# Group states of a Mamba-2 SSD layer: B and the weighted x in a high and a low part, three rounded products in place of plain 32-bit ones, for groups 1 to 7

## The chip, the cores and the metric

The kernel runs on one core of one Trainium2 chip. A core has four compute engines and a queue engine, each of which works off its own list of instructions in the order of that list: PE (TensorE, matrix products into PSUM), DVE (VectorE), ACT (ScalarE), POOL (GpSimd, which here also issues a few DMAs) and SP (which issues the weight loads). Engines wait for each other through semaphores. The metric is the time of one execution in microseconds of the device; 0.2% of this kernel's time, 2 us, is about what a measurement can tell from no change.

## The reference

One layer mixes 256 latent tokens, with 256 context tokens as prefix, by a bidirectional Mamba-2 scan of 8 groups of 4 heads and by a gated MLP. The part at hand is the state of a chunk of 128 tokens, per direction, and the output that is read from it:

```python
acs = jnp.cumsum(a, axis=2)
decay_to_end = jnp.exp(a_tot[:, :, None] - acs)
states = jnp.einsum('bckgn,bckgr,bckgrp->bcgrpn', Bc, decay_to_end, xdt)
...
hT, h_starts = lax.scan(step, h0, (states, a_tot))
...
CB = jnp.einsum('bcqgn,bckgn->bcgqk', Cc, Bc)
y_diag = jnp.einsum('bcgqk,bcgrqk,bckgrp->bcqgrp', CB, Lmat, xdt)
y_off = jnp.einsum('bcqgn,bcgrpn,bcqgr->bcqgrp', Cc, h_starts, jnp.exp(acs))
```

A group's state is a product of B (tokens by 128) with x, each token of x weighted by its decay. B, C and x come from the input projection through a depthwise convolution of width 5 and SiLU.

## The kernel before

The input projection makes 32 channel tiles of 128 channels (for group g: tiles 4g and 4g+1 are x, 4g+2 is B, 4g+3 is C, for which the latent tokens alone are computed). Seven tiles are made in a first stage, the other 25 in the stage with which the change is concerned, from 130 to 432 us: PE adds up 16 steps of k into the PSUM tile `psx`. Each step is three products of numbers in the rounded 32-bit form (`float32r`): a weight w is split into a high part `hi_w` (ACT, a cast) and a low part `lo_w` (DVE, w minus the high part), and high times high, high times low and low times high are summed (`mm3`, lines 139 to 143). The activations stand split in `hhi` and `hlo`. Splits run three half tiles ahead of PE (`split_hi`, `split_lo`, lines 492 to 502).

Between these products the recurrence of the groups runs, by a clock written out by hand: `later(dt, fn)` files a piece of work under a due time, `pump` moves the clock forward by 1.3 for two steps of k (0.65 for a tile of latent tokens) and issues what is due. On PE, DVE, ACT and POOL the instructions stand in the order in which `pump` issues them. Of a tile i (`plan_tile`, line 877) come in turn:

- the convolution (`conv_tile`): ACT starts the sum from `psx` (`tap0`, line 560), DVE adds four taps (line 576), ACT applies SiLU (line 579). The exponential of the decays, `E` (line 743, ACT), needs another table than SiLU, so ACT loads tables in between (ACT_TABLE_LOAD, at lines 579 and 743);
- of an x tile, a transposition on PE (`ptx`, line 695) and a copy to `xk` (`ssd_xc`, line 699, ACT); after the second x tile of a group, `ssd_w` on POOL: four products of `xk` with decays make `xw` (context tokens, line 707), two make `xl` (latent tokens, line 710);
- of a B tile, a transposition (`ptb`, line 718) and a copy to `bk` (line 723, ACT);
- after the C tile, the recurrence of the group: on PE `pcb` (C times B, line 761), `psc` and `psl` (the states, lines 778 and 781, plain 32-bit products, each of which the trace shows as two passes), then `hs` (the states joined: ACT line 788, POOL line 794, DVE line 800), `M` (POOL line 806 and DVE line 814), `E` times M (line 816), `pso` (line 831), `yo` (DVE line 837), the sum of `yo` into `y` (POOL line 845), `psy` (line 857), `yc` (ACT line 864) and `pty` (line 871).

The rows R of decays of the next group are loaded by a DMA that POOL issues (line 677) once `ssd_min` (line 737, DVE) has read those of the group before. `cv1` is a pool with one buffer for each tag, so a tile with the same tag waits until the one before has been read.

Of the kernel before, what the change touches and what calls it, by code (L numbers as in the profile page):

```python
# [44 lines left out]
def tile_hybrid_ssd_mlp(  # L45
# [116 lines left out]
    zt, e = yseg(5)[:, 0:256], yseg(5)[:, 256:512]  # L162
# [9 lines left out]
    def spt(shape, name):  # L172
        return sps.tile(shape, F32, tag="s", name=name)
# [136 lines left out]
    for k in range(KT):  # L310
# [5 lines left out]
        g = k % 4  # L316
        nc.tensor.matmul(pss[32 * g : 32 * g + 32, :], lhsT=ones[:, 0:32], rhs=sq, start=k < 4, stop=k >= KT - 4)
        if g == 3:
            warm(512)
            if k < 12:  # L320
# [7 lines left out]
                     start=True, stop=True)  # L328
# [141 lines left out]
    cv1 = cvs.enter_context(mkpool(name="cv1", bufs=1))  # L470
# [76 lines left out]
    def conv_tile(i, src, d0, ds):  # L547
        ch = ORDER[i]
        lat = ch >= 24
        n = 256 if lat else 512  # L550
        cw = pc[:, C_CW + 5 * i : C_CW + 5 * i + 5]
        l0 = 0 if lat else 256
        T = {}

        def tap0():
            if ch < 16:
                o = cv3.tile([P, n], F32, tag="xs", name=f"xbc{i}")
            else:
                o = cv2.tile([P, n], F32, tag="cs" if lat else "bs", name=f"xbc{i}")
            nc.scalar.activation(o, src, AF.Identity, bias=pc[:, C_CB + i : C_CB + i + 1], scale=cw[:, 2:3])  # L560
            T["o"] = o

        def taps():
            o = T["o"]
            o4 = o[:, l0 : l0 + 256].rearrange("p (r t) -> p r t", r=4)
            src4 = src[:, l0 : l0 + 256].rearrange("p (r t) -> p r t", r=4)
            for k in (0, 1, 3, 4):
                s = k - 2
                parts = [(o4, src4, 64)]
                if not lat:  # L570
                    parts.append((o[:, 0:256], src[:, 0:256], 256))
                for (a, z, w) in parts:
# [3 lines left out]
                    nc.vector.scalar_tensor_tensor(ao, zi, cw[:, k : k + 1], ao, op0=ALU.mult, op1=ALU.add)  # L576

        def silu():
            nc.scalar.activation(T["o"], T["o"], AF.Silu)
# [102 lines left out]
    gs_ = {}  # L682

    def hp(ap):
        return ap.rearrange("p (h q) -> p h q", h=4)

    def ssd_x(g, xi):
        S = gs_.setdefault(g, {})
        if xi == 0:
            S["xk"] = cv2.tile([P, 4, 256], F32, tag="xk", name=f"xk{g}")  # L690
        xk = S["xk"]
        xt = done.pop(4 * g + xi)
        p = spt([P, 4, P], f"ptx{g}{xi}")
        for t in range(4):
            nc.tensor.transpose(p[:, t, :], xt[:, t * P : (t + 1) * P], ident)
        S["ptx", xi] = p

    def ssd_xc(g, xi):
        nc.scalar.copy(gs_[g]["xk"][:, :, xi * P : (xi + 1) * P], gs_[g]["ptx", xi])

    def ssd_w(g):
        S = gs_[g]
        xk, h4 = S["xk"], slice(4 * g, 4 * g + 4)
        xw = cv1.tile([P, 2, 2, 256], F32, tag="xw", name=f"xw{g}")
        for t in range(2):
            for d in range(2):
                nc.gpsimd.tensor_tensor(hp(xw[:, t, d, :]), hp(xk[:, t, :]), bc(wctx(t, d)[:, h4], 2, 64), op=ALU.mult)
        xl = cv1.tile([P, 2, 256], F32, tag="xl", name=f"xl{g}")
        for d in range(2):
            nc.gpsimd.tensor_tensor(hp(xl[:, d, :]), hp(xk[:, 2 + d, :]), bc(wlt(d)[:, h4], 2, 64), op=ALU.mult)  # L710
        S["xw"], S["xl"] = xw, xl

    def ssd_b(g):
        bt = done[4 * g + 2]
        bk = cv1.tile([P, 4, P], F32, tag="bk", name=f"bk{g}")
        p = spt([P, 4, P], f"ptb{g}")
        for t in range(4):
            nc.tensor.transpose(p[:, t, :], bt[:, t * P : (t + 1) * P], ident)
# [54 lines left out]
    def ssd_states(g):  # L773
        S = gs_[g]
        bk, xw, xl = S["bk"], S["xw"], S["xl"]
        psc = spt([P, 2, 256], f"psc{g}")
        for t in range(2):
            nc.tensor.matmul(psc, lhsT=bk[:, t, :], rhs=xw[:, t], start=t == 0, stop=t == 1)  # L778
        psl = spt([P, 2, 256], f"psl{g}")
        for d in range(2):  # L780
            nc.tensor.matmul(psl[:, d, :], lhsT=bk[:, 2 + d, :], rhs=xl[:, d, :], start=True, stop=True)
# [307 lines left out]
    for blk in range(16):  # L1089
# [83 lines left out]
    for i in range(8):  # L1173
        tk, b = divmod(i, 4)
# [5 lines left out]
    xf = [load_raw(xtok[tk], f"xf{tk}") for tk in range(2)]  # L1180
# [148 lines left out]
```

## Time and profile before

| | |
|---|---|
| median of 3 runs | 990.47 us (990.31 to 990.49) |
| the profiled execution's own time | 989.67 us |
| its span, first to last instruction | 987.9 us |
| busy: PE, DVE, ACT, POOL | 978.8, 621.4, 495.4, 112.5 us |
| granted clock of PE, mean | 0.999 |

The profile is of one execution. Its page gives each engine's busy time, the chain of work that ended last, and groups of instructions by line; the trace behind it can be asked for a stretch of time, for one line, or for the waits. In a timeline a row has the start in us, the time taken, engine, line, operation, tile written and tiles read; in brackets stands how long the engine had been idle and which work ended that. A matrix product's end is modelled, so the time from its start to the start of the next one is what it costs PE. Rows of equal instructions that follow each other are put together (x4).

### The profile page before, as it was taken

To read this page: it belongs to the slowest core of one execution; us is meant where nothing else is said; L and a number is where in the kernel's file an instruction comes from. 1 tells how busy PE (TensorE), PEld (TensorE's weight loads), DVE (VectorE), ACT (ScalarE), POOL (GpSimd) and SP (SyncE) were. 2 spreads that over 40 slices of the span, in tenths; PEclk is the share of its full clock that TensorE was granted. 3 is DMA by queue.
4 is the path that set the end of the run, shared out by engine and by line. 5 is a ranking of instruction groups with operands and counts; after the bars stand their busy time and mean duration, and the time that the engine had idled before them with its cause. 6 is when DMAs were issued, how large, how long until landed. Compare 5 with 4: busy or idle time off the path is not lost.

```text
span 987.9 us, 13929 instructions
## 1 busy us (share of the span) xinstructions
PE 978.8 (99%) x5502; PEld 792.6 (80%) x5502; DVE 621.4 (63%) x949; ACT 495.4 (50%) x762; POOL 112.5 (11%) x162
## 2 busy tenths in 40 slices
PE   9999999999999999999999999999999999999997
PEld 4688888778887878787888888887888888888885
DVE  4444488868886566756767766767555564445636
ACT  4233358566665554545445343454565563346522
POOL 0000002432453222224000000000000000000000
PEclk9999999999999999999999999999999999999999
DMA  9999844233323424145877768774455446556722
GB/s 372 421 418 418 352 149 166 86 129 128 128 75 139 142 98 145 43 169 206 297 302 284 275 257 296 280 274 170 170 180 203 171 170 213 178 206 228 282 86 85
DMA packets 31985, 207.26 MB, mean 210 GB/s; under 512 B 4128, under 2 KB 4384, under 8 KB 8496
## 3 DMA queue, kind: packets, MB, share of 16 engines
q1 hardware_dynamic: 29232, 192.79, 52.0%
q0 software_dynamic: 2112, 12.65, 3.7%
q8 instruction: 43, 0.70, 0.3%
q10 hardware_dynamic: 576, 0.94, 0.3%
q14 instruction: 22, 0.18, 0.1%
HBM read 204.20 MB, written 2.16 MB: 209 GB/s over the span
## 4 chain that ended last, share of the span: by engine, by line
PE 92%; DMA 4%; ACT 2%; DVE 1%; SPq 0%; issue 0%; ACTq 0%
PE pa L1108 12%; PE pa L1110 12%; PE pa L1109 12%; PE psx L141 9%; PE psx L143 9%; PE psx L142 9%; PE pm L1157 3%; PE pm L1155 3%; PE pm L1156 3%; DMA wst<-in_wst_dram 3%; PE pq L1157 2%; PE pq L1156 2%; PE pq L1155 2%; PE psada L249 2%; PE psc L778 1%; PE pso L831 1%
## 5 line engine op out<-in xcount | busy, mean ns | idle before, releaser
L85 DVE TENSOR_TENSOR lo_w<-w,hi_w 128x1024 fp32r<-128x1024 f32 x173 | 210.7, 1224 | 146.0 <-ACT hi_w L84 145.9
L84 ACT CAST hi_w<-w 128x1024 fp32r<-128x1024 f32 x173 | 182.1, 1053 | 204.5 <-PE pa L1110 129.4
L1108 PE MATMUL pa<-hi_w,hhi 128*128 128x512 f32 x512 | 202.3, 395 | 0.0
L1110 PE MATMUL pa<-hi_w,hlo 128*128 128x512 f32 x512 | 199.5, 390 | 0.0
L1109 PE MATMUL pa<-lo_w,hhi 128*128 128x512 f32 x512 | 199.3, 389 | 0.0
L141 PE MATMUL psx<-hhi,hi_w 128*128 128x512 f32 (+1 forms) x400 | 153.4, 383 | 0.0
L143 PE MATMUL psx<-hhi,lo_w 128*128 128x512 f32 (+1 forms) x400 | 145.9, 365 | 0.0
L142 PE MATMUL psx<-hlo,hi_w 128*128 128x512 f32 (+1 forms) x400 | 145.7, 364 | 0.0
L1108 PEld LDWEIGHTS pa<-hi_w,hhi 128*128 128x128 f32 x512 | 96.2, 188 | 20.5 <-issue 1.6
L1110 PEld LDWEIGHTS pa<-hi_w,hlo 128*128 128x128 f32 x512 | 96.1, 188 | 20.3
L1109 PEld LDWEIGHTS pa<-lo_w,hhi 128*128 128x128 f32 x512 | 96.2, 188 | 19.5 <-issue 0.2
L576 DVE SCALAR_TENSOR_TENSOR xbc<-psx,pc,xbc 128x248 f32<-128x248 f32 (+1 forms) x204 | 83.6, 473 | 34.8 <-ACT xbc L560 33.9
L501 DVE TENSOR_TENSOR lo_w<-w,hi_w 128x1024 fp32r<-128x1024 f32 x61 | 77.1, 1271 | 23.7 <-ACT hi_w L495 23.6
L141 PEld LDWEIGHTS psx<-hhi,hi_w 128*128 128x128 f32 x400 | 75.5, 189 | 13.4 <-issue 2.9
L143 PEld LDWEIGHTS psx<-hhi,lo_w 128*128 128x128 f32 x400 | 75.4, 188 | 12.5
L142 PEld LDWEIGHTS psx<-hlo,hi_w 128*128 128x128 f32 x400 | 75.6, 189 | 12.2 <-issue 1.7
L495 ACT CAST hi_w<-w 128x1024 fp32r<-128x1024 f32 x61 | 63.5, 1044 | 26.0 <-PE psx L142 12.9
L966 DVE SCALAR_TENSOR_TENSOR junk<-gate,cb 128x2048 bf16<-128x2048 f32 x16 | 36.7, 2291 | 24.1 <-DMA gate<-in_wada_dram 24.1
L1155 PE MATMUL pm<-hi_w,hhi 128*128 128x512 f32 x128 | 50.0, 390 | 0.0
L1156 PE MATMUL pm<-lo_w,hhi 128*128 128x512 f32 x128 | 49.9, 390 | 0.0
L1157 PE MATMUL pm<-hi_w,hlo 128*128 128x512 f32 x128 | 49.7, 389 | 0.0
L730 ACT ACTIVATE R<-R,y 128x128 f32<-128x128 f32 x128 | 38.8, 391 | 0.0
(248 smaller groups left out, 1333.6 us busy)
## 6 DMA issues: line engine op xcount, KB each, us to landing
w<-in_wlat_dram SPq DMA_DIRECT2D x64, 1024.0 KB, 4.8
w<-in_wout_dram SPq DMA_DIRECT2D x32, 1024.0 KB, 4.8
ada<-in_wada_dram SPq DMA_DIRECT2D x30, 1024.0 KB, 13.4
w<-in_wxbc_dram SPq DMA_DIRECT2D x25, 1024.0 KB, 4.8
gate<-in_wada_dram SPq DMA_DIRECT2D x16, 1024.0 KB, 5.5
R<-acs POOLq DMA_DIRECT2D x8, 1024.0 KB, 5.2
wst<-in_wst_dram SPq DMA_DIRECT2D x15, 480.0 KB, 14.0
xT<-in_xch_dram SPq DMA_DIRECT2D x4, 1024.0 KB, 8.0
```

Of the source, the lines that this page charges most:

```text
L84: nc.scalar.copy(hi, raw)
L85: nc.vector.tensor_tensor(lo, raw, hi.bitcast(F32), op=ALU.subtract)
L141: nc.tensor.matmul(ps, lhsT=whi, rhs=hhi[k][:, s], start=start, stop=False)
L142: nc.tensor.matmul(ps, lhsT=whi, rhs=hlo[k][:, s], start=False, stop=False)
L143: nc.tensor.matmul(ps, lhsT=wlo, rhs=hhi[k][:, s], start=False, stop=stop)
L576: nc.vector.scalar_tensor_tensor(ao, zi, cw[:, k : k + 1], ao, op0=ALU.mult, op1=ALU.add)
L1108: nc.tensor.matmul(pa[tk], lhsT=hhi[k][:, t], rhs=whi[:, w], start=k == 0, stop=False)
L1109: nc.tensor.matmul(pa[tk], lhsT=hhi[k][:, t], rhs=wlo[:, w], start=False, stop=False)
L1110: nc.tensor.matmul(pa[tk], lhsT=hlo[k][:, t], rhs=whi[:, w], start=False, stop=k == KT - 1)
L1155: nc.tensor.matmul(p, lhsT=yh[:, t], rhs=whi[:, w], start=j == 0, stop=False)
L1156: nc.tensor.matmul(p, lhsT=yh[:, t], rhs=wlo[:, w], start=False, stop=False)
L1157: nc.tensor.matmul(p, lhsT=yl[:, t], rhs=whi[:, w], start=False, stop=hf == 0 and j == 15)
```

## The change

For groups 1 to 7 B and the weighted x are split as the weights are: ACT casts to a high part, DVE subtracts it to get a low part. Each plain product of `psc` and `psl` becomes three rounded ones (high by high, high by low, low by high). POOL now writes one half at a time of the weighted x into a buffer `xf`, which has one copy: part n=0 and n=1 are the two context chunks, n=2 the latent ones. `ssd_w(g, n)` (POOL) and `ssd_ws(g, n)` (ACT cast, DVE subtraction) alternate, 2.7 units of the clock between parts. So POOL's part n+1 waits until ACT and DVE have read part n, and ACT's cast waits for POOL. The tiles share tags with others: the high and the low part of `xl` take those of `yo`, `hs` that of the low part of `xw`. Group 0 is computed as before. Some due times move: the C tiles with `late` of 10 in the early calls get 12, `tw` (from the transposed x to `ssd_w`) becomes 17 for tile 5 and 6 for tile 17, and the product with the skip weight, `ssd_sk`, comes after the three parts.

```diff
-    def ssd_w(g):
+    def ssd_w(g, n):
         S = gs_[g]
+        if g == 0:
+            if n == 0:
+                S["xw"] = cv1.tile([P, 2, 2, 256], F32, tag="xw0", name="xw")
+                S["xl"] = cv1.tile([P, 2, 256], F32, tag="yo0", name="xl")
+            xf = S["xl"] if n == 2 else S["xw"][:, n]
+        elif n == 0:
+            S["xw"] = [cv1.tile([P, 2, 2, 256], F32R, tag=f"xw{v}", name=f"xw{v}{g}") for v in range(2)]
+        if g and n == 2:
+            S["xl"] = [cv1.tile([P, 2, 256], F32R, tag=f"yo{v}", name=f"xl{v}{g}") for v in range(2)]
         xk, h4 = S["xk"], slice(4 * g, 4 * g + 4)
-        xw = cv1.tile([P, 2, 2, 256], F32, tag="xw", name=f"xw{g}")
-        for t in range(2):
-            for d in range(2):
-                nc.gpsimd.tensor_tensor(hp(xw[:, t, d, :]), hp(xk[:, t, :]), bc(wctx(t, d)[:, h4], 2, 64), op=ALU.mult)
-        xl = cv1.tile([P, 2, 256], F32, tag="xl", name=f"xl{g}")
+        if g:
+            S["xf"] = xf = cv1.tile([P, 2, 256], F32, tag="xf", name=f"xf{g}{n}")
         for d in range(2):
-            nc.gpsimd.tensor_tensor(hp(xl[:, d, :]), hp(xk[:, 2 + d, :]), bc(wlt(d)[:, h4], 2, 64), op=ALU.mult)
-        S["xw"], S["xl"] = xw, xl
+            nc.gpsimd.tensor_tensor(hp(xf[:, d, :]), hp(xk[:, 2 + d if n == 2 else n, :]),
+                                    bc((wlt(d) if n == 2 else wctx(n, d))[:, h4], 2, 64), op=ALU.mult)
+
+    def ssd_ws(g, n):
+        S = gs_[g]
+        if g == 0:
+            return
+        hi, lo = S["xl"] if n == 2 else [v[:, n] for v in S["xw"]]
+        nc.scalar.copy(hi, S["xf"])
+        nc.vector.tensor_tensor(lo, S["xf"], hi.bitcast(F32), op=ALU.subtract)
...
     def ssd_bc(g):
-        nc.scalar.copy(gs_[g]["bk"], gs_[g]["ptb"])
+        hi, lo = (gs_[g]["bk"] + [None])[:2]
+        nc.scalar.copy(hi, gs_[g]["ptb"])
+        if g == 0:
+            return
+        nc.vector.tensor_tensor(lo, gs_[g]["ptb"], hi.bitcast(F32), op=ALU.subtract)
...
+        parts = ((0, 0), (0, 1), (1, 0))
+        if g == 0:
+            parts, xw, xl = ((0, 0),), [xw], [xl]
+        e = len(parts) - 1
         for t in range(2):
-            nc.tensor.matmul(psc, lhsT=bk[:, t, :], rhs=xw[:, t], start=t == 0, stop=t == 1)
+            for n, (a, b) in enumerate(parts):
+                nc.tensor.matmul(psc, lhsT=bk[a][:, t, :], rhs=xw[b][:, t], start=t + n == 0, stop=t == 1 and n == e)
...
         if r == 1:
-            later(d0 + tx + tw, lambda: ssd_w(g))
-            later(d0 + tx + tw + 3, lambda: ssd_sk(g))
+            for n in range(3):
+                later(d0 + tx + tw + 2.7 * n, lambda n=n: ssd_w(g, n))
+                later(d0 + tx + tw + 2.7 * n + 1.3, lambda n=n: ssd_ws(g, n))
+            later(d0 + tx + tw + 7.5, lambda: ssd_sk(g))
...
         if i < 8:
-            plan_tile(i, ps, ds=7, tx=11.5 if i == 4 else 9, tw=12, late=10)
+            plan_tile(i, ps, ds=7, tx=11.5 if i == 4 else 9, tw=17 if i == 5 else 12, late=12)
         else:
-            plan_tile(i, ps, td=1.3 if i < 12 else 0)
+            plan_tile(i, ps, td=1.3 if i < 12 else 0, tw=6 if i == 17 else 1.5)
```

Where the instructions move, three places show. In the rows the first number behind a name is the tile's own (xbc19 is channel tile 19, xf42 is part 2 of group 4, xw04 the high part of group 4, hi_w29 a half tile of weights); what follows the underscore is a buffer, which differs between the two programs. Lines are those of each program's own code: L725 and L726 are the new cast and subtraction, L717 is POOL's weighting, L739 and L742 the split of B.

The first place is ACT before the states of group 1. Before:

```order
L864 COPY yc0_2095<-psy0_2078 128x512
L743 ACT_TABLE_LOAD
L743 ACTIVATE E1_2097<-E1_2097 128x1024
L579 ACT_TABLE_LOAD
L579 ACTIVATE xbc8_2074<-xbc8_2074 128x512
L495 CAST hi_w14_2138<-w7_1890 128x1024
L788 COPY hs1_2169<-psc1_2143 128x2x256
```

And now:

```order
L890 COPY yc0_2092<-psy0_2075 128x512
L725 CAST xw01_2068<-xf10_2070 128x512
L762 ACT_TABLE_LOAD
L762 ACTIVATE E1_2094<-E1_2094 128x1024
L725 CAST xw01_2068<-xf11_2115 128x512
L579 ACT_TABLE_LOAD
L579 ACTIVATE xbc8_2066<-xbc8_2066 128x512
L495 CAST hi_w14_2142<-w7_1890 128x1024
L725 CAST xl01_2144<-xf12_2146 128x512
```

The three casts of group 1 stand among the exponential, the SiLU of tile 8 and the weight cast; in the old order POOL had all of group 1's weighting done earlier, ahead of M01. On PE the places of `pcb1`, `psc1` and `psl1` move from step 10 of tile 9 to step 12, behind `ptx20`; `pso1` from step 2 to step 6 of tile 10.

The second place is the same stretch of group 4, on ACT and on POOL. ACT before:

```order
L864 COPY yc3_2981<-psy3_2966 128x512
L579 ACTIVATE xbc18_2906<-xbc18_2906 128x512
L560 ACTIVATE xbc19_3010<-psx19_2899,pc_87 128x256
L495 CAST hi_w29_3012<-w14_2739 128x1024
L743 ACT_TABLE_LOAD
L743 ACTIVATE E4_2983<-E4_2983 128x1024
L723 COPY bk4_3033<-ptb4_3034 128x512
L579 ACT_TABLE_LOAD
L579 ACTIVATE xbc19_3010<-xbc19_3010 128x256
```

ACT now:

```order
L890 COPY yc3_3039<-psy3_3024 128x512
L725 CAST xw04_3009<-xf40_3011 128x512
L579 ACTIVATE xbc18_2961<-xbc18_2961 128x512
L560 ACTIVATE xbc19_3070<-psx19_2954,pc_87 128x256
L495 CAST hi_w29_3075<-w14_2785 128x1024
L762 ACT_TABLE_LOAD
L762 ACTIVATE E4_3041<-E4_3041 128x1024
L725 CAST xw04_3009<-xf41_3072 128x512
L739 CAST bk04_3098<-ptb4_3100 128x512
L725 CAST xl04_3113<-xf42_3115 128x512
L579 ACT_TABLE_LOAD
L579 ACTIVATE xbc19_3070<-xbc19_3070 128x256
```

The SiLU of tile 19, which `pcb4` reads, now stands behind all three casts. POOL before:

```order
L806 TENSOR_TENSOR M31_2870<-cbb3_2819,dtt_1483 128x512
L707 TENSOR_TENSOR xw4_2872<-xk4_2751,ed_1484 128x256 x4
L710 TENSOR_TENSOR xl4_2877<-xk4_2751,ed_1484 128x256 x2
L823 TENSOR_TENSOR y_68<-xk4_2751,dsk_109 128x256 x2
L845 TENSOR_TENSOR y_68<-y_68,yo30_2916 128x256 x2
L845 TENSOR_TENSOR y_68<-y_68,yo31_2938 128x256 x2
L677 DMA R5_2994<-acs_1485 128x2048
```

POOL now:

```order
L871 TENSOR_TENSOR y_68<-y_68,yo31_2991 128x256 x2
L717 TENSOR_TENSOR xf40_3011<-xk4_2802,ed_1484 128x256 x2
L677 DMA R5_3054<-acs_1485 128x2048
L717 TENSOR_TENSOR xf41_3072<-xk4_2802,ed_1484 128x256 x2
L717 TENSOR_TENSOR xf42_3115<-xk4_2802,ed_1484 128x256 x2
L849 TENSOR_TENSOR y_68<-xk4_2802,dsk_109 128x256 x2
```

The weighting of group 4 has moved behind the sum of `yo31` and around the load of R5. On DVE the six instructions around it read, in order: the weight split lo_w27, the first `ssd_min` of E4, the subtraction for xf40, lo_w28, the second `ssd_min` of E4 (for which R5's load waits), the taps of tile 19; then the sum of `pty3`, the subtraction for xf41, lo_w29, the low part of B, the subtraction for xf42.

The third place is ACT ahead of the B tile of group 5; groups 6 and 7 have the same order. Before:

```order
L699 COPY xk5_3215<-ptx51_3302 128x4x128
L560 ACTIVATE xbc22_3335<-psx22_3244,pc_87 128x512
L495 CAST hi_w35_3337<-w17_3059 128x1024
L495 CAST hi_w36_3377<-w18_3190 128x1024
L579 ACTIVATE xbc22_3335<-xbc22_3335 128x512
```

And now:

```order
L699 COPY xk5_3299<-ptx51_3386 128x4x128
L725 CAST xw05_3398<-xf50_3400 128x512
L560 ACTIVATE xbc22_3418<-psx22_3328,pc_87 128x512
L495 CAST hi_w35_3420<-w17_3135 128x1024
L725 CAST xw05_3398<-xf51_3428 128x512
L495 CAST hi_w36_3463<-w18_3274 128x1024
L725 CAST xl05_3471<-xf52_3473 128x512
L579 ACTIVATE xbc22_3418<-xbc22_3418 128x512
```

The SiLU of tile 22, which `ptb5` reads, stands behind the cast of part 2. Groups 2 and 3 have the pattern too: in group 2 the SiLU of tile 10 (read by `ptb2`) comes behind the cast of xf22, in group 3 the SiLU of tile 16 (read by `ptx40`) behind that of xf31. On DVE the subtraction for xf21 stands behind the taps of tile 10 and lo_w17, the one for xf30 behind the taps of tile 16 and lo_w23, the one for xf51 behind the taps of tile 22 and lo_w35.

More of the change, by code (lines that the diff above doesn't have):

```diff
@@ L699, in ssd_xc @@
         nc.scalar.copy(gs_[g]["xk"][:, :, xi * P : (xi + 1) * P], gs_[g]["ptx", xi])
-    def ssd_w(g):
+    def ssd_w(g, n):
         S = gs_[g]
-        xk, h4 = S["xk"], slice(4 * g, 4 * g + 4)
-        xw = cv1.tile([P, 2, 2, 256], F32, tag="xw", name=f"xw{g}")
-        for t in range(2):
-            for d in range(2):
-                nc.gpsimd.tensor_tensor(hp(xw[:, t, d, :]), hp(xk[:, t, :]), bc(wctx(t, d)[:, h4], 2, 64), op=ALU.mult)
-        xl = cv1.tile([P, 2, 256], F32, tag="xl", name=f"xl{g}")
-        for d in range(2):
-            nc.gpsimd.tensor_tensor(hp(xl[:, d, :]), hp(xk[:, 2 + d, :]), bc(wlt(d)[:, h4], 2, 64), op=ALU.mult)
-        S["xw"], S["xl"] = xw, xl
+        if g == 0:
[7 more added lines that the diff above has]
+            S["xl"] = [cv1.tile([P, 2, 256], F32R, tag=f"yo{v}", name=f"xl{v}{g}") for v in range(2)]
+        xk, h4 = S["xk"], slice(4 * g, 4 * g + 4)
+        if g:
+            S["xf"] = xf = cv1.tile([P, 2, 256], F32, tag="xf", name=f"xf{g}{n}")
+        for d in range(2):
+            nc.gpsimd.tensor_tensor(hp(xf[:, d, :]), hp(xk[:, 2 + d if n == 2 else n, :]),
[7 more added lines that the diff above has]
+        nc.vector.tensor_tensor(lo, S["xf"], hi.bitcast(F32), op=ALU.subtract)
     def ssd_b(g):
         bt = done[4 * g + 2]
-        bk = cv1.tile([P, 4, P], F32, tag="bk", name=f"bk{g}")
+        bk = [cv1.tile([P, 4, P], F32R if g else F32, tag=f"bk{v}", name=f"bk{v}{g}") for v in range(2 if g else 1)]
         p = spt([P, 4, P], f"ptb{g}")
@@ L776, in ssd_states @@
         psc = spt([P, 2, 256], f"psc{g}")
+        parts = ((0, 0), (0, 1), (1, 0))
+        if g == 0:
+            parts, xw, xl = ((0, 0),), [xw], [xl]
+        e = len(parts) - 1
         for t in range(2):
-            nc.tensor.matmul(psc, lhsT=bk[:, t, :], rhs=xw[:, t], start=t == 0, stop=t == 1)
+            for n, (a, b) in enumerate(parts):
+                nc.tensor.matmul(psc, lhsT=bk[a][:, t, :], rhs=xw[b][:, t], start=t + n == 0, stop=t == 1 and n == e)
         psl = spt([P, 2, 256], f"psl{g}")
         for d in range(2):
-            nc.tensor.matmul(psl[:, d, :], lhsT=bk[:, 2 + d, :], rhs=xl[:, d, :], start=True, stop=True)
+            for n, (a, b) in enumerate(parts):
+                nc.tensor.matmul(psl[:, d, :], lhsT=bk[a][:, 2 + d, :], rhs=xl[b][:, d, :], start=n == 0, stop=n == e)
         S["psc"], S["psl"] = psc, psl
@@ L786, in ssd_hc @@
         S = gs_[g]
-        S["hs"] = cv1.tile([P, 2, 2, 256], F32, tag="hs", name=f"hs{g}")
+        S["hs"] = cv1.tile([P, 2, 2, 256], F32, tag="xw1", name=f"hs{g}")
         nc.scalar.copy(S["hs"].rearrange("p c d x -> p (c d) x")[:, 0:4:3, :], S["psc"])
```

## The prediction

> **What bounds the kernel now.** I read the page first, for busy time and for the chain that ended last.
>
> ```profile
> PE 978.8 (99%) x5502; PEld 792.6 (80%) x5502; DVE 621.4 (63%) x949; ACT 495.4 (50%) x762; POOL 112.5 (11%) x162
> ...
> PE 92%; DMA 4%; ACT 2%; DVE 1%; SPq 0%; issue 0%; ACTq 0%
> ```
>
> PE is busy for 978.8 of 987.9 us and carries 92% of the chain. A mean over the span can hide idle stretches, so I then read the windows: length, busy time of PE, PEld, DVE, ACT and POOL with their counts, granted clock, DMA share, GB/s.
>
> ```profile
> 260.00:300.00 40.00, 40.00 (x214) 32.79 (x213) 29.88 (x56) 24.77 (x41) 19.25 (x24) 1.00 0.33 120
> 980.00:985.00 5.00, 1.81 (x4) 0.30 (x2) 3.21 (x7) 1.79 (x5) 0.00 (x0) 1.00 0.34 127
> 985.00:987.90 2.90, 0.00 (x0) 0.00 (x0) 0.00 (x0) 0.00 (x0) 0.00 (x0) 0.53 0.39 143
> ```
>
> In 260 to 300, where the recurrence of groups 3 and 4 runs, PE is busy for 40.00 of 40.00 us. So in the stretch of the change nothing but PE's list sets the time: PE work removed there shortens the kernel by its full price, and work added elsewhere is free as long as PE never meets an operand that isn't ready. Where it does, the wait lengthens the kernel by its full length. The timeline gives PE's prices (start, time, engine, line, operation), from the start of one group of products to the next.
>
> ```profile
> 199.91 0.60 PE L761 MATMUL pcb<-xbc,xbc 128*128 128x128 f32 x4
> 200.35 1.88 PE L778 MATMUL psc<-xw,bk 128*128 128x512 f32 x4
> 202.07 1.03 PE L781 MATMUL psl<-xl,bk 128*128 128x256 f32 x4
> 203.17 0.40 PE L142 MATMUL psx<-hlo,hi_w 128*128 128x512 f32 x1
> 203.40 0.39 PE L143 MATMUL psx<-hhi,lo_w 128*128 128x512 f32 x1
> ...
> 286.56 0.28 PE L143 MATMUL psx<-hhi,lo_w 128*128 128x256 f32 x1
> 286.68 0.28 PE L141 MATMUL psx<-hhi,hi_w 128*128 128x256 f32 x1
> ```
>
> `psc` starts at 200.35 and the product behind `psl` at 203.17. A rounded product takes 203.40 − 203.17 = 0.23 with 512 columns and 286.68 − 286.56 = 0.12 with 256.
>
> **The change part by part.** PE. The two plain products of `psc` and the two of `psl` cost 203.17 − 200.35 = 2.82 less the 0.23 of one product still in the pipeline (the last product's end overlaps the next start), 2.59. Six rounded products of 512 columns and six of 256 cost 6 × 0.23 + 6 × 0.12 = 2.1. The gain is 0.5 per group, 3.5 for seven. All of it counts, as PE sets the end.
>
> The other engines. The new operations don't occur before; their nearest rows do (forms apart: count, busy time and mean ns of one; for L707 the shortest, middle and longest).
>
> ```profile
> L707 POOL TENSOR_TENSOR xw<-xk,ed x32: 602/612/1591, 164.3 to 426.2; 128x256 f32<-128x256 f32 x32
> L511 ACT CAST hhi<-w 128x512 fp32r<-128x512 f32 x16 | 9.0, 617 | 5.1 <-DMA w<-in_wout_dram 5.1
> L512 DVE TENSOR_TENSOR hlo<-w,hhi 128x512 fp32r<-128x512 f32 x16 | 10.2, 687 | 3.3 <-ACT hhi L511 3.3
> L495 ACT CAST hi_w<-w 128x1024 fp32r<-128x1024 f32 x61 | 63.5, 1044 | 26.0 <-PE psx L142 12.9 <-PE pa L1110 12.9
> L501 DVE TENSOR_TENSOR lo_w<-w,hi_w 128x1024 fp32r<-128x1024 f32 x61 | 77.1, 1271 | 23.7 <-ACT hi_w L495 23.6
> L579 ACT ACT_TABLE_LOAD x9 | 11.5, 1283 | 7.6 <-DVE xbc L576 7.6
> L579 ACT ACTIVATE xbc<-xbc 128x512 f32<-128x512 f32 x24 | 15.1, 628 | 5.1 <-DVE xbc L576 5.1
> ```
>
> A cast of 128x512 takes 0.62, a subtraction 0.69, so per group ACT gets three casts (1.9; the copy of B merely becomes a cast) and DVE four subtractions (2.8). ACT is busy 50% of the span, DVE 63%: as load this is hidden by PE's products. As order it is not. One `xf` makes each group a chain: POOL writes a part (2 × 0.6 = 1.2), ACT casts it (0.6), DVE subtracts (0.65), and only then may POOL start the next. Every link stands in a list behind other work. So I follow each list to the next thing PE needs. Starts in a list lie some 0.05 to 0.1 closer than durations say, as 291.12 (0.68) followed by 291.72 shows below; I count 0.6 to 0.65 for short operations and 1.15 for `lo_w`.
>
> Group 1.
>
> ```profile
> 197.26 0.69 DVE L737 TENSOR_TENSOR E<-R 128x512 f32<-128x512 f32 x1
> 198.47 0.59 POOL L677 DMA_DIRECT2D R<-acs  x1 [4.33 <-issue]
> ```
>
> The second `ssd_min` ended at 197.95 and R2's load was issued 0.5 later. Now the subtraction for xf10 is ahead of that `ssd_min`: +0.6, so POOL is free of the load at 198.47 + 0.6 + 0.6 = 199.7. Then xf11 1.2, its cast 0.6 (201.5), on ACT the table 1.3, SiLU 0.6, hi_w14 1.0 (204.4), on DVE lo_w14 1.15 (205.6), and the last subtraction, for xf12: 206.2. PE comes to `psc1` after two more steps of tile 9 (6 × 0.23 = 1.4), ptx20 and `pcb1` (0.44 each by 200.35 − 199.91): 199.9 + 1.4 + 0.9 = 202.2, and with 1.36 of `psc1` to `psl1` at 203.5. **PE waits 2.7** (2.2 with each step a tenth shorter, 3.2 if the xf12 pair of POOL is held for 0.5).
>
> Group 2. The SiLU of tile 10, which `ptb2` needs, is now behind the cast of xf22.
>
> ```profile
> 219.32 0.59 ACT L699 COPY xk<-ptx 128x512 f32<-128x512 f32 x1 [1.38 <-PE ptx L695]
> 221.22 1.06 ACT L743 ACTIVATE E<-E 128x1024 f32<-128x1024 f32 x1
> 222.53 0.78 ACT L560 ACTIVATE xbc<-psx,pc 128x512 f32<-128x512 f32 x1 [0.25 <-PE psx L143]
> 223.35 3.20 DVE L576 SCALAR_TENSOR_TENSOR xbc<-psx,pc,xbc 128x248 f32<-128x248 f32 x8 [1.45 <-ACT xbc L560]
> 227.91 0.63 ACT L579 ACTIVATE xbc<-xbc 128x512 f32<-128x512 f32 x1
> 230.83 0.60 PE L718 MATMUL ptb<-ident,xbc 128*128 128x128 f32 x4
> ```
>
> `xk2` is ready at 219.9; xf20 1.2, cast 0.6 (221.7), table 1.3, E2 1.05, tap0 0.75 (224.8), the taps of tile 10 3.2, lo_w17 1.15 (229.15), the subtraction for xf21 0.65 (229.8), xf22 1.2, cast 0.6, table 1.3, SiLU 0.6: 233.6. It ended at 228.5 before; PE wants it at 230.83. **2.8** (2.2 by shorter steps, 3.9 if POOL's last pair is held by a `lo_w`).
>
> Group 3. ptx40 needs the SiLU of tile 16, now behind the cast of xf31.
>
> ```profile
> 263.82 1.36 DVE L501 TENSOR_TENSOR lo_w<-w,hi_w 128x1024 fp32r<-128x1024 f32 x1
> 266.30 0.60 PE L695 MATMUL ptx<-ident,xbc 128*128 128x128 f32 x4
> ```
>
> lo_w23 ends at 265.2; low part of B 0.6, subtraction for xf30 0.65, xf31 1.2, cast 0.6, SiLU 0.6: 268.8 against 266.30. **2.5** (1.9 to 3.0).
>
> Group 4. `pcb4` needs the SiLU of tile 19, now behind three casts.
>
> ```profile
> 280.86 1.13 DVE L814 SCALAR_TENSOR_TENSOR M<-cbf,dtt,M 128x128 f32<-128x128 f32 x4
> 283.93 2.54 DVE L814 SCALAR_TENSOR_TENSOR M<-cbf,dtt,M 128x128 f32<-128x128 f32 x4 [1.22 <-POOL M L806]
> 291.12 0.68 DVE L837 TENSOR_TENSOR yo<-pso,ed 128x512 f32<-128x512 f32 x1
> 291.72 1.21 DVE L501 TENSOR_TENSOR lo_w<-w,hi_w 128x1024 fp32r<-128x1024 f32 x1
> 291.88 4.80 POOL L845 TENSOR_TENSOR y<-y,yo 128x256 f32<-128x256 f32 x2 [1.27 <-DVE yo L837]
> 300.34 0.60 PE L761 MATMUL pcb<-xbc,xbc 128*128 128x128 f32 x4
> ```
>
> The weighting moves away from `M31`: its four operations took 2.54 with POOL at work beside them and take 1.13 alone (280.86), so yo31 comes 1.4 earlier, and 0.5 by group 3's gain on PE: 291.8 − 1.9 = 289.9. The sum of yo31 on POOL took 4.80 for two operations of 0.6 while DVE ran `lo_w` and the `ssd_min` of E: I take it as held through lo_w27 and E4 (1.8), then 1.2: 292.9. xf40 294.1, cast 294.7, subtraction 295.35, lo_w28 296.5, second `ssd_min` 297.1, the issue of R5's load 1.1 (298.2), xf41 299.4, cast 300.0, subtraction 300.65, xf42 held by lo_w29 303.0, cast 303.6, table 304.9, SiLU 0.4: 305.3. PE wants it at 300.34 − 0.5 = 299.8. **5.5** (2.5 if POOL is never held, 6.0).
>
> Groups 5 to 7. `ptb5` needs the SiLU of tile 22, now behind the cast of xf52.
>
> ```profile
> 334.64 3.19 DVE L576 SCALAR_TENSOR_TENSOR xbc<-psx,pc,xbc 128x248 f32<-128x248 f32 x8 [3.96 <-ACT xbc L560]
> 337.75 2.35 DVE L501 TENSOR_TENSOR lo_w<-w,hi_w 128x1024 fp32r<-128x1024 f32 x2
> 342.14 0.60 PE L718 MATMUL ptb<-ident,xbc 128*128 128x128 f32 x4
> ```
>
> Taps end 337.8, lo_w35 1.15, subtraction for xf51 0.65 (339.6), xf52 1.2 and held by lo_w36 for 1.15 (341.95), cast 0.6, SiLU 0.6: 343.15 against 342.14. **1.0 each** (0 without the hold, 1.3).
>
> The holds are read off the rows: POOL's operation takes 0.60 mostly and 1.59 at worst, and the 4.80 above lies beside DVE's two-input operations. [...] Counted by bare durations instead, groups 5 to 7 would wait for nothing and group 4 for 2.5.
>
> **The sum.** 2.7 + 2.8 + 2.5 + 5.5 + 3 × 1.0 = 16.5 of waits, less 3.5: +13.0. Made against the profiled execution: 989.67 + 13.0 = 1002.7. The median of the runs, 990.47, stands 0.8 above it: **1003.5**. With the low ends the waits are 2.2 + 2.2 + 1.9 + 2.5 = 8.8, with the high ones 3.2 + 3.9 + 3.0 + 6.0 + 3.9 = 20.0: 996 to 1007 is this case's own range. Each wait is paid anew, since each chain starts with a product of PE (ptx21 for group 2) and so moves with PE.
>
> **Rivals.** *The chains are ready in time: faster.* It turns at each place on the time between two products of PE: in group 2 the chain has 230.83 − 219.9 = 10.9 us, and I count 13.7. If the lists let the links overlap after all (POOL's parts ahead of the table load and the taps), only the PE gain is left: 990.47 − 3.5 = 987.0. For it: no engine but PE is over 63% busy. Against: eight links on three ordered lists, each with a row. Faster begins where the waits together stay under 1.5.
>
> *The wait is paid once.* After group 1's 2.7 every other engine is ahead of PE by as much, and weight splits or loads that now run earlier leave the lists clear. −3.5 + 2.7: 989.7, no change. Against: the chains start at PE's own products.
>
> *The clock falls in the waits.* In the windows above the clock is 1.00 through 980 to 985 and 0.53 after 985, once PE had been busy for only 1.81 of 5 us. If each wait over 2 us were followed by as long a stretch at half the clock, half of 13.5 is lost besides: up to 6.7, so 1004 to 1010, say 1008. [...] The trace agrees that the clock falls at idle, but has no wait in mid-stage to show the price.
>
> *Rounded products are no cheaper here.* Then the 3.5 is missing: 1007. Against: 0.23 and 0.12 are what these very forms cost in the same stage.
>
> **How the numbers follow.** Waits at PE as worked out 0.56 (1003.5), with the clock 0.17 (1008), rounded not cheaper 0.04 (1007): slower 0.77. Paid once 0.08: same. Ready in time 0.15: faster. 0.2%, 2 us, is about what a measurement can tell, so the same is 988.5 to 992.5. The range goes from 989, the paid-once case, to 1010, the clock's end, and leaves out the 0.15 below and little above.
>
> **What would show it.** In the profile after: PE's groups of `psc` and `psl` at 0.23 and 0.12 a product, 2.1 per group; PE idle some 16 us between 200 and 435, ahead of `psl1` (2.7), `ptb2` (2.8), ptx40 (2.5), `pcb4` (5.5) and ptb5 to ptb7 (1.0), with ACT (SiLU) named as what ended it, at `psl1` DVE; POOL's weighting at L717 with waits for DVE before each part; the clock at 1.00 in the windows of the waits, or below for that rival. The prediction is wrong if the SiLU of tile 10 ends within 11 us of `xk2`, if PE is busy throughout, or if the groups wait and the time still doesn't rise.

## The result, and the profile after

| | before | after |
|---|---|---|
| median | 990.39 us (4 runs, 989.57 to 990.49) | 1008.02 us (4 runs, 1007.42 to 1008.09) |
| span of the profiled execution | 987.9 us | 1006.3 us |
| granted clock of PE, mean | 0.999 | 0.992 |

The change makes the kernel slower: ratio 1.0179, 95% interval 1.0164 to 1.0194. The forecast was 1003.5 in a range of 989 to 1010. On the page, DVE and ACT have the splits' work and PE is at 98%. Of the chain that ended last the page now places only 70% of the span, PE has 65% (92% before), and POOL is new in it.

```profile
PE 982.8 (98%) x5530; PEld 799.1 (79%) x5530; DVE 637.7 (63%) x977; ACT 506.6 (50%) x783; POOL 116.3 (12%) x162
...
PE 65%; DVE 2%; POOL 1%; ACT 1%; issue 1%; DVEq 0%; ACTq 0%
```

The view of PE's waits names who ended them (line waited, releaser, us in total, times, longest). Before, only ptx, 0.5, was there of these three.

```profile
PE pcb L780 <- ACT xbc L579: 5.3, 1, 5.3
PE ptb L733 <- ACT xbc L579: 4.9, 4, 2.9
PE ptx L695 <- ACT xbc L579: 4.4, 3, 2.1
```

All three are SiLU on ACT. PE's timeline has the places; of each pair of rows the first is the last product ahead of the wait.

```profile
201.23 0.39 PE L143 MATMUL psx<-hhi,lo_w 128*128 128x512 f32 x1
203.71 0.66 PE L695 MATMUL ptx<-ident,xbc 128*128 128x128 f32 x4 [2.09 <-ACT xbc L579]
...
234.50 0.39 PE L143 MATMUL psx<-hhi,lo_w 128*128 128x512 f32 x1
237.74 0.66 PE L733 MATMUL ptb<-ident,xbc 128*128 128x128 f32 x4 [2.85 <-ACT xbc L579]
...
274.17 0.39 PE L143 MATMUL psx<-hhi,lo_w 128*128 128x512 f32 x1
276.36 0.66 PE L695 MATMUL ptx<-ident,xbc 128*128 128x128 f32 x4 [1.80 <-ACT xbc L579]
...
309.74 0.39 PE L143 MATMUL psx<-hhi,lo_w 128*128 128x512 f32 x1
315.43 1.22 PE L780 MATMUL pcb<-xbc,xbc 128*128 128x128 f32 x4 [5.30 <-ACT xbc L579]
...
358.99 0.39 PE L143 MATMUL psx<-hhi,lo_w 128*128 128x512 f32 x1
360.07 0.66 PE L733 MATMUL ptb<-ident,xbc 128*128 128x128 f32 x4 [0.69 <-ACT xbc L579]
```

A product costs 0.23 from start to start, so the waits are 203.71 − 201.23 − 0.23 = 2.25 (group 1), 3.0 (group 2), 2.0 (group 3), 5.5 (group 4) and 0.85 (group 5; groups 6 and 7 the same): 15.2 in all. That doesn't reach the 18.4 by which the span grew, and 3.5 of gain has still to be taken off. The rest is in the windows, cut at the times at which the clock changed (length, busy PE, PEld, DVE, ACT, POOL, granted clock, DMA share, GB/s):

```profile
201.16:204.57 3.41, 1.32 (x11) 0.90 (x10) 0.69 (x1) 3.38 (x5) 2.05 (x4) 1.00 0.94 382
204.57:207.98 3.41, 3.41 (x13) 2.83 (x12) 2.57 (x4) 1.48 (x4) 1.31 (x2) 0.50 0.17 72
235.29:238.70 3.41, 0.96 (x7) 0.88 (x7) 3.41 (x7) 3.38 (x5) 1.31 (x2) 1.00 0.51 214
238.70:242.12 3.42, 3.42 (x10) 2.65 (x9) 3.31 (x7) 1.71 (x4) 0.00 (x0) 0.50 0.00 0
272.84:276.25 3.41, 1.72 (x8) 1.10 (x6) 1.46 (x3) 1.09 (x3) 1.19 (x2) 1.00 0.53 156
...
310.38:313.80 3.42, 0.00 (x0) 0.00 (x0) 2.30 (x4) 0.95 (x3) 2.90 (x4) 1.00 0.58 177
313.80:317.21 3.41, 1.78 (x6) 1.69 (x7) 1.75 (x2) 2.50 (x3) 0.34 (x1) 0.50 0.61 255
317.21:320.62 3.41, 3.41 (x12) 2.93 (x12) 1.06 (x4) 0.59 (x1) 1.75 (x3) 0.50 0.00 0
```

Behind three of the four long waits the clock is 0.50, for 3.4, 3.4 and 6.8 us. Products there start 0.43 apart:

```profile
239.11 0.63 PE L141 MATMUL psx<-hhi,hi_w 128*128 128x512 f32 x1
239.54 0.63 PE L142 MATMUL psx<-hlo,hi_w 128*128 128x512 f32 x1
```

PE had work for 3.4, 3.4 and, from 315.43 on, 5.2 of these, 12.0 in all; of each 0.43, 0.43 − 0.23 = 0.20 is lost, so 5.6. The sum: 15.2 of waits + 5.6 of clock − 3.5 = 17.3, and 0.3 where a tile of group 2 begins late (231.90, 0.45 behind a product of 0.12, released by the taps): 17.6 of 18.4. The other 0.8 is not placed.

### The profile page after: what moved, and what is told of

Read it like the earlier page. It is cut to its first block, busy times and chain, and to the rows that moved or that the text cites. A ratio compares the mean times of both kernels' runs of the same rounds, so it can differ in the third digit from the quotient of the medians.

```text
span 1006.3 us, 14018 instructions
## 1 busy us (share of the span) xinstructions
PE 982.8 (98%) x5530; PEld 799.1 (79%) x5530; DVE 637.7 (63%) x977; ACT 506.6 (50%) x783; POOL 116.3 (12%) x162
## 4 chain that ended last, share of the span: by engine, by line
PE 65%; DVE 2%; POOL 1%; ACT 1%; issue 1%; DVEq 0%; ACTq 0%
PE pa L1136 12%; PE pa L1138 11%; PE pa L1137 11%; PE psx L141 3%; PE pm L1185 3%; PE pm L1184 3%; PE pm L1183 3%; PE psx L143 3%; PE psx L142 3%; PE pq L1185 2%; PE pq L1184 2%; PE pq L1183 2%; POOL xf L717 1%; DVE xbc L576 1%; PE psg L1078 1%; PE pso L857 1%
```

## The experiments

The theory: one `xf` and lists in order make SiLU wait behind casts that wait for POOL. The rivals that could give such a result are load (DVE and ACT have too much to do), products that are no cheaper, and a wait at the subtractions rather than at SiLU; the clock is a cost on top. Each kernel ran beside runs of the kernel before on the same chip, whose median is in brackets.

**e1, a second buffer.**

```diff
-            S["xf"] = xf = cv1.tile([P, 2, 256], F32, tag="xf", name=f"xf{g}{n}")
+            S["xf", n] = xf = cv1.tile([P, 2, 256], F32, tag=f"xf{n % 2}", name=f"xf{g}{n}")
```

> The changed kernel, with two buffers for xf in place of one (part n in buffer n modulo 2), nothing else changed. Theory: the waits of PE come from the chain through the one buffer. With two, POOL's part 2 needs only the subtraction of part 0. By the changed kernel's own rows the SiLU of tile 10 then ends at 234.1 in place of 237.7 (PE wants it at 234.7), that of tile 16 at 272.7 (274.4), that of tile 22 at 356.0 (359.2): the waits at ptb2 (3.0), ptx40 (2.0) and ptb5 to ptb7 (0.85 each) go, and the drop of the clock at ptb2 (1.6) with them. At ptx20 nothing changes, since POOL's xf11 there stands behind the load of R2; at pcb4 5.5 becomes about 3, as xf41 stands behind the load of R5. So 1008.0 - 3.0 - 2.0 - 2.6 - 1.6 - 2.4 = 996.4, and 1 or 2 less if the clock falls for a shorter time at pcb4. Rival, load: ACT and DVE have too much to do in all; the buffer then changes little, 1005 to 1008.

Measured: 996.56 us (994.88 to 997.76; before 989.9). The waits at ptb2, ptx40 and ptb5 to ptb7 are gone, ptx20 has its 2.25 still, `pcb4` 3.1. So of the 15.2 us of waits 9.9 hung on the one buffer. Unforeseen was a new wait of 1.55 at `pcb2`. The clock fell once in the profile, behind `pcb4` (0.50 from 308.14 to 311.56), and not at ptx20 (1.00 from 198.92 to 205.75), which the sum had left in; this and the new wait cancel, so that the number came so close is in part luck.

**e2, the cast of part 2 behind SiLU.**

```diff
-                later(d0 + tx + tw + 2.7 * n + 1.3, lambda n=n: ssd_ws(g, n))
+                later(d0 + tx + tw + 2.7 * n + (1.9 if n == 2 else 1.3), lambda n=n: ssd_ws(g, n))
```

> The changed kernel, with the cast and subtraction of part 2 filed 0.6 units of the clock later, so that on ACT the SiLU of tiles 10, 22, 26 and 30 stands ahead of the cast it was behind. One buffer as before. Theory, order of the list: ptb2 waits no more (3.0, and 1.6 of clock), ptb5 to ptb7 neither (0.85 each); ptx20, ptx40 and pcb4 stay as they are: 1008.0 - 7.2 = 1000.8. Rival, the split's work itself is late: then psl2 and psl5 to psl7 wait in place of the transpositions, and the time stays within 2 of 1008.

Measured: 1005.82 us (1004.22 to 1006.36): a miss. Groups 5 to 7 lost their waits as expected. In group 2 ptb2 waits no more, but `pcb2`, six steps later, waits 3.0, for the SiLU of tile 11, and the clock is 0.50 from 240.77 to 244.18. Rows of e2 on DVE, ACT and PE:

```profile
232.34 4.66 DVE L576 SCALAR_TENSOR_TENSOR xbc<-y,pc,xbc 128x248 f32<-128x248 f32 x8
...
240.75 0.42 ACT L579 ACTIVATE xbc<-xbc 128x256 f32<-128x256 f32 x1 [3.03 <-DVE xbc L576]
...
241.22 1.22 PE L780 MATMUL pcb<-xbc,xbc 128*128 128x128 f32 x4 [2.84 <-ACT xbc L579]
```

The taps of tile 11 stand on DVE behind those of tile 12, which took 4.66 while POOL ran xf22 and the skip weight, and two subtractions, one on each side of these. In group 2 there were two late chains one behind the other, and the wait at ptb2 had hidden the second. The rival's own sign, waits at psl2 and psl5 to psl7, is missing; whether tile 11 is late by load or by order, e2 can't tell (e8 does).

**e3, PE kept busy in the waits.**

```diff
+    def fill(p, n):
+        w = 512 if len(p.shape) == 3 and p.shape[1] == 4 else 256
+        for _ in range(n):
+            nc.tensor.matmul(p, lhsT=hhi[0][:, 0:P], rhs=hhi[1][:, 0:w], start=True, stop=True)
...
+        if (g, xi) == (2, 0):
+            fill(p, 8)
...
+        if g == 2:
+            fill(p, 11)
...
+        if g == 4:
+            fill(pcb, 40)
```

> The changed kernel, with rounded products on PE that nobody reads, put into the three long waits: 8 of 512 columns ahead of ptx20 (1.8 us of a wait of 2.25), 11 ahead of ptb2 (2.5 of 3.0), 40 of 256 columns ahead of pcb4 (4.8 of 5.5), into the PSUM tile that the awaited work writes next. The waits stay, but PE is busy in them. Theory, the clock is a cost of its own: it stays at 1.00, and its three drops (3.4, 3.4 and 6.8 us at half rate, of which PE was busy for 3.4, 3.4 and 5.2, half of it lost: 6.0) go: 1008.0 - 6.0 = 1002.0. Rival, what is missing is in the waits or in slower products of the new form: the time stays at 1008 or rises.

Measured: 1003.94 us (1003.70 to 1005.18; before 989.9): 14.0 above the kernel before, where the changed kernel is 17.6 above it, so PE does 59 products more in 3.6 us less. The clock is 1.00 in the windows of the three filled waits (200 to 210, 234 to 244 and 306 to 322), and its mean over the span is 0.998 in place of 0.992. That the clock is a cost of its own is shown; what comes back is less than the 6.0 expected. Half was too much, as worked out above: 5.6. And waits that the slow clock had covered now show. One is at the second product of `psl1`:

```profile
206.47 0.28 PE L818 MATMUL psl<-xl,bk 128*128 128x256 f32 x1
207.03 0.86 PE L818 MATMUL psl<-xl,bk 128*128 128x256 f32 x5 [0.27 <-DVE xl L733]
```

It is 207.03 − 206.47 − 0.12 = 0.44, for the last subtraction, where the prediction had put all of group 1's wait. Another 0.3 lies within `psc2`'s six products (from its start to that of `psl2` 1.79 in place of 1.46), and the late tile of group 2 begins 0.2 later than it did: 5.6 − 0.44 − 0.3 − 0.2 = 4.7. In the two profiles e3's stage is 4.4 shorter: its last `pty` starts at 473.50 in place of 477.43, and at 112 us it had been 0.43 later than the changed kernel. The rest is within what runs differ by.

**e4, the products alone** (`xl`, `bk` and `psl` are edited like `xw` and `psc`).

```diff
-        xw = cv1.tile([P, 2, 2, 256], F32, tag="xw", name=f"xw{g}")
+        xw = cv1.tile([P, 2, 2, 256], F32R if g else F32, tag="xw", name=f"xw{g}")
...
-            nc.tensor.matmul(psc, lhsT=bk[:, t, :], rhs=xw[:, t], start=t == 0, stop=t == 1)
+            for n in range(3 if g else 1):
+                nc.tensor.matmul(psc, lhsT=bk[:, t, :], rhs=xw[:, t], start=t + n == 0, stop=t == 1 and n == (2 if g else 0))
```

> The kernel before, in its own order, with POOL writing xw and xl and ACT writing bk of groups 1 to 7 directly in the rounded form, and three rounded products of the same two operands in place of each plain one. It leaves out the low parts and their splits: no cast, no subtraction, no xf; the products of the high parts are counted three times. Theory: PE's gain is 7 x 0.5 = 3.5 and there is no wait: 990.4 - 3.5 = 986.9. Rival, three rounded products are no cheaper than a plain one: 990.4. If POOL is slower in writing the rounded form, or the clock or a split is disturbed, something between or above.

Measured: 986.2 us (985.96 to 986.23; before 989.9): a ratio of 0.9960 (0.9945 to 0.9975), 3.7 us. The gain on PE is real and as large as worked out.

**e5, group 1's order (with two buffers).** The due times of POOL's parts, the casts, the subtractions and the skip weight, in units of the written clock (`ssd_ws` casts when its last argument is 0 and subtracts when it is 1):

```diff
+    DUE = {
+        1: ((46.8, 46.9, 49.5), (48.1, 49.9, 52.05), (48.9, 50.35, 52.2), 54.3),
+    }
...
+        if r == 1 and g in DUE:
+            w, c, s, sk = DUE[g]
+            for n in range(3):
+                later(w[n] - now[0], lambda n=n: ssd_w(g, n))
+                later(c[n] - now[0], lambda n=n: ssd_ws(g, n, 0))
+                later(s[n] - now[0], lambda n=n: ssd_ws(g, n, 1))
```

> Two buffers for xf, and for group 1 alone other due times: POOL's part 1 ahead of the load of R2, both casts ahead of the exponential, both subtractions behind the second minimum of E1 (which R2's load waits for), part 2's cast ahead of hi_w14. Theory: at ptx20 the SiLU of tile 8 was behind a cast that waited for POOL, and POOL for the load of R2; the wait of 2.25 goes, 996.6 - 2.25 = 994.3, and up to 1.7 less in those runs in which the clock fell there. Rival: the wait is the last subtraction's (as the prediction had it, at psl1): then PE waits there instead and the time stays at 996 to 997.

Measured: 994.19 us (993.86 to 994.49; before 990.07). The 2.25 at ptx20 is gone and nothing takes its place, at `psl1` neither: the order around this SiLU was the cause. The run moves POOL's part 1, the casts and the subtractions together; that it was POOL's part 1 behind the load of R2 is read from the rows of the changed kernel (below), not varied alone.

**e6 and e7, groups 2 and 4 too.** Two more lines in the table; e7 has plain products of the high parts in the same order.

```diff
+        2: ((65.7, 66.2, 67.8), (67.45, 67.75, 70.9), (67.75, 73.75, 75.35), 67.9),
+        4: ((112.5, 112.6, 119.0), (116.8, 116.9, 120.3), (118.95, 122.15, 122.2), 124.5),
```

> Group 1 as in the run beside it, and other due times for groups 2 and 4 too: in group 2 POOL's three parts follow each other during the taps that read PSUM, the first cast stands behind the exponential, and two of the subtractions behind the taps of tile 11; in group 4 POOL's first two parts follow M31 directly, as in the kernel before, and part 2 the load of R5. All splits and all three products are done. Theory: nothing is left of the waits but what the lists force, so the gain of the products shows: 990.4 - 3.5 = 986.9, clock at 1.00, faster than both kernels. Rival, load: DVE's 2.8 and ACT's 1.9 us per group leave a wait at pcb2 (1.5 with two buffers) or pcb4 (3.1): 988.5 to 991.

> The kernel of the run beside it (all casts and subtractions done, groups 1, 2 and 4 with the other due times), with plain 32-bit products of the high parts alone in place of the three rounded ones; it leaves out the low parts in the products. Theory: the same order and the same work on ACT, DVE and POOL, PE 0.5 slower per group: 3.5 above that run, about 990.4, level with the kernel before. That would show the split itself to cost nothing where its order is right. Rival: the split costs time of its own; above 991.

Measured: e6 991.26 us (989.57 to 992.08, 11 runs; before 990.07, ratio 1.0011, 1.0002 to 1.0020), e7 993.28 us (992.11 to 994.77). e6 is a miss by 4.4. In group 2 `psc2` alone waits 0.4, for the low part of B. In group 4 `pcb4` still waits 2.4; rows of e6 on POOL and ACT:

```profile
291.32 5.41 POOL L873 TENSOR_TENSOR y<-y,yo 128x256 f32<-128x256 f32 x2 [2.14 <-DVE yo L865]
...
297.28 2.24 POOL L717 TENSOR_TENSOR xf<-xk,ed 128x256 f32<-128x256 f32 x2
...
299.55 0.62 ACT L726 CAST xl<-xf 128x512 fp32r<-128x512 f32 x1 [3.15 <-POOL xf L717]
...
301.97 0.42 ACT L579 ACTIVATE xbc<-xbc 128x256 f32<-128x256 f32 x1
```

The new table had left the cast of part 2 ahead of the SiLU of tile 19, and POOL's part 2 behind a sum of 5.41. It is the same mechanism, once more, at a place where the rival had a wait too; e8 tells the two apart. The runs are spread with the clock: seven at a mean of 0.996 or 0.997 took 991.0 to 992.1, four at 0.998 or 0.999 took 989.6 to 991.5. e7 stands 2.0 above e6, not 3.5; `psc2`'s 0.4 can't occur in it, and the spread by the clock can cover the rest, so this pair decides nothing.

**e8 and e9, the order mended.**

```diff
-        2: ((65.7, 66.2, 67.8), (67.45, 67.75, 70.9), (67.75, 73.75, 75.35), 67.9),
-        4: ((112.5, 112.6, 119.0), (116.8, 116.9, 120.3), (118.95, 122.15, 122.2), 124.5),
+        2: ((65.7, 66.2, 67.8), (67.45, 67.75, 70.9), (67.75, 75.32, 75.35), 67.9),
+        4: ((112.5, 112.6, 119.0), (116.8, 116.9, 124.85), (118.95, 120.95, 124.95), 124.5),
```

> The reordered kernel with two more due times: in group 4 the cast and the subtraction of part 2 stand behind the SiLU of tile 19 (and the subtraction of part 1 ahead of lo_w29), in group 2 the low part of B stands ahead of the subtraction for xf21. Theory: in the reordered kernel the SiLU of tile 19 was still behind a cast that waited for POOL (2.4 at pcb4, and in some runs 1.7 of clock), and psc2 waited 0.4 for the low part of B. Both go: no wait is left, 990.1 - 3.5 = 986.6, and the runs lie close together, as the clock no longer falls in some of them. Rival, load: the subtraction of part 2 is late for psl4 instead, 988 to 990.

> The kernel of the run beside it, casts and subtractions all done, with plain 32-bit products of the high parts alone; it leaves out the low parts in the products. Theory: 3.5 above that run, level with the kernel before (990.1): the split is hidden where its order is right, and the three rounded products are the whole gain. Rival: the split has a price of its own, over 991.

Measured: e8 986.81 us (986.58 to 988.14; before 990.34), ratio 0.9964 (0.9952 to 0.9977); e9 990.43 us (ratio 1.0000, 0.9990 to 1.0009). Every split and all three products are in e8, and it beats both kernels, by 3.5 and 21. e9, the same splits in the same order with plain products, is level with the kernel before: the split costs nothing where the order is right, and the products are the whole gain. The page of e8 and its waits of PE:

```profile
PE 975.3 (99%) x5530; PEld 794.7 (81%) x5530; DVE 639.3 (65%) x977; ACT 506.7 (51%) x783; POOL 115.7 (12%) x162
```

```profile
PE ptx L695 <- ACT xbc L579: 0.5, 1, 0.5
```

In the stage only the 0.5 is left that the kernel before has as well. DVE and ACT do as much as in the changed kernel (637.7 and 506.6), so load was not its limit.

## Why the prediction was right, and where it was not

- **PE's gain, 3.5:** right; 3.7 in e4, 3.5 between e8 and the kernel before. (The 0.23 that the working takes off is the first product on `psx` behind `psl`, which starts at 202.75; the one at 203.17 is the second.)
- **Waits, 16.5:** right in mechanism, 15.2 measured. Group 2: 2.8 said, 3.0 measured; group 3: 2.5 and 2.0 (the low part of B, counted into the chain with 0.6, stood further ahead on DVE, at 265.58); group 4: 5.5 and 5.5; groups 5 to 7: 1.0 and 0.85. The chain of group 2 can be read link by link in the timeline after, of ACT, DVE and POOL in turn:

```profile
226.80 1.06 ACT L762 ACTIVATE E<-E 128x1024 f32<-128x1024 f32 x1
...
235.13 0.62 ACT L725 CAST xl<-xf 128x512 fp32r<-128x512 f32 x1 [3.50 <-POOL xf L717]
...
237.06 0.63 ACT L579 ACTIVATE xbc<-xbc 128x512 f32<-128x512 f32 x1
```

```profile
228.56 3.19 DVE L576 SCALAR_TENSOR_TENSOR xbc<-psx,pc,xbc 128x248 f32<-128x248 f32 x8 [1.75 <-ACT xbc L560]
231.67 1.22 DVE L501 TENSOR_TENSOR lo_w<-w,hi_w 128x1024 fp32r<-128x1024 f32 x1
232.80 0.68 DVE L726 TENSOR_TENSOR xw<-xf,xw 128x512 fp32r<-128x512 f32 x1
```

```profile
233.57 1.53 POOL L717 TENSOR_TENSOR xf<-xk,ed 128x256 f32<-128x256 f32 x2 [6.08 <-DVE xw L726]
```

  Exponential, taps, `lo_w`, subtraction, POOL, cast, SiLU: POOL sat idle for 6.08 until the subtraction released its one buffer. That the 2.8 came so close is in part luck: from the end of `xk2`'s copy (222.20) to the end of this SiLU the chain took 15.5, not 13.7, as the sum of `yo` on POOL (218.84, 3.91) made xf20 late; but PE was due 12.5 behind `xk2`, not 10.9, as `psy1` now stands behind ptx21. The largest wait, group 4's, has the links that were foretold; of POOL and ACT in turn:

```profile
299.80 3.06 POOL L871 TENSOR_TENSOR y<-y,yo 128x256 f32<-128x256 f32 x2 [2.14 <-DVE yo L863]
...
307.64 0.59 POOL L677 DMA_DIRECT2D R<-acs  x1 [3.64 <-issue]
...
310.90 2.10 POOL L717 TENSOR_TENSOR xf<-xk,ed 128x256 f32<-128x256 f32 x2 [1.46 <-DVE xw L726]
```

```profile
313.03 0.62 ACT L725 CAST xl<-xf 128x512 fp32r<-128x512 f32 x1 [2.45 <-POOL xf L717]
...
314.96 0.42 ACT L579 ACTIVATE xbc<-xbc 128x256 f32<-128x256 f32 x1
```

  From the end of the sum of yo31 (302.86) to the end of this SiLU (315.38) it took 12.5; the prediction's links have 12.4.
- **Group 1's place:** wrong. The step had the wait of 2.7 at `psl1`, for the last subtraction. It was 2.25 at ptx20, for the SiLU of tile 8. The prediction's own links have this SiLU end at 203.4 and ptx20 due at 201.3; it never set the two against each other. That 2.7 and 2.25 are close is luck. In the changed kernel's rows the cast ahead of the SiLU waits for POOL's part 1, which follows the load of R2:

```profile
199.26 0.59 POOL L677 DMA_DIRECT2D R<-acs  x1 [5.95 <-issue]
199.87 1.20 POOL L717 TENSOR_TENSOR xf<-xk,ed 128x256 f32<-128x256 f32 x2
```

```profile
201.10 0.62 ACT L725 CAST xw<-xf 128x512 fp32r<-128x512 f32 x1 [1.27 <-POOL xf L717]
201.74 1.28 ACT L579 ACT_TABLE_LOAD   x1
203.03 0.63 ACT L579 ACTIVATE xbc<-xbc 128x512 f32<-128x512 f32 x1
```

  Of the wait at `psl1` there is 0.4, and only at full clock (e3).
- **POOL held by DVE:** right in the times. POOL's pair for the last part of group 5 took 2.10 in place of 1.2, with DVE's lo_w36 beside it (356.58, 1.22), and e6's sum 5.41, with two weight splits, two `ssd_min` and a subtraction beside it (291.16 to 295.31). The pair for xf40 took 1.18 (302.82) while DVE was idle. That DVE's operations hold POOL's is read from such rows; no run varied it alone.

```profile
356.74 2.10 POOL L717 TENSOR_TENSOR xf<-xk,ed 128x256 f32<-128x256 f32 x2 [4.07 <-DVE xw L726]
```

- **The clock:** the failed step. The forecast set it aside at 0.17, yet three drops came on top of the waits, 5.6 us by the rows (3.6 is what e3 gives back). With waits 1.3 shorter than said, they make up about the 4.5 between 1003.5 and 1008.0; the rival had "up to 6.7" and 1008. That rival's condition, as long a stretch at half the clock behind each wait over 2 us, was an assumption, and the rows show it in part: behind the waits of 2.25, 3.0 and 5.5 the clock was 0.50 for 3.4, 3.4 and 6.8 us, behind the one of 2.0 it stayed at 1.00. By the rows a drop of 3.4 us costs 1.6.
- **Paid once; hidden; no cheaper:** none of them came. Each group paid anew, until the order was changed (e8).

## What to carry to other kernels

Work that is free as load can cost its whole length as order: follow each new instruction to what stands behind it in its list and on to the next thing the bounding engine reads, and set every consumer on that way against its own due time, not the last one alone. A staging buffer with one copy between three engines turns three free operations into one chain; a second copy gave back 11 us here before any order was touched. Where PE is the bound, a wait can cost more than its own length: here one of 2.25 us was followed by 3.4 us at half clock, 1.6 more.

## What the runs showed of the hardware

In the profile of the changed kernel the clock falls at 204.57, 238.70 and 313.80 and is back at 207.98, 242.12 and 320.62: from each of these times to the next it is a whole number of 3.41 us (1, 9, 1, 21 and 2). Cut into stretches of 3.41 by these times, PE's busy share in the stretch ahead of a fall was 0.39, 0.28 and 0.00 (1.32, 0.96 and 0.00 of 3.41); behind a share of 0.50 (1.72, from 272.84) the clock stayed at 1.00. In two other profiles it fell behind 0.30 (e2, 1.02 from 237.36) and 0.24 (e1, 0.82 from 304.73). In e2 the same wait of 2.25 at ptx20 lay otherwise across such stretches and the clock stayed at 1.00, with 0.46 busy:

```profile
199.81:203.22 3.41, 1.57 (x7) 0.95 (x6) 0.69 (x1) 2.33 (x3) 1.95 (x4) 1.00 1.00 368
```

So in these rows the clock fell behind shares of up to 0.39 and stayed behind 0.46 and 0.50; no run varied the share by itself. That a wait of 2 to 3 us costs some 1.7 more (half of 3.41) or nothing by how it lies across such stretches, and that this makes the spread of e1, e2 and e6, is the author's estimate. It fits the runs of e1, of which one at a mean clock of 0.999 took 994.9 and three at 0.996 took 996.2 to 997.8. Behind a stretch at 0.50 with 0.52 busy (1.78, from 313.80) the clock was 0.50 for another; behind the full ones it was 1.00 again, and behind one with 0.87 (e2, 2.96 from 240.77) products start 0.23 apart again.

DVE took longer beside POOL too, but not always. The taps of tile 12, which read `y`, took 4.66 in e2 (from 232.34), with POOL at work beside them for 3.04 (from 232.50), and 3.23 in e6, where POOL was idle; the taps of tile 10, which read `psx`, took 3.20 in the kernel before (from 223.35) while POOL weighted the x of group 2 (221.84 to 225.31). What makes the difference no run varied.

```profile
228.18 3.23 DVE L576 SCALAR_TENSOR_TENSOR xbc<-y,pc,xbc 128x248 f32<-128x248 f32 x8
```

POOL writes the rounded form at no price that shows: in e4 its products of 128x256 for `xw`, 28 of 32 of them rounded, have a median of 614 ns, before 612.
